# A decoder block with gathered and dense experts: gate loads and gate products held in the order of the program, and four steps of the gathered experts given high priority

## The chip, the cores and the metric

The kernel runs on one core of one Trainium2 chip. The metric is device time in microseconds (us) for one execution: the median of three runs for the time, one further profiled execution for the trace.

## The reference

One decoder layer for 1024 tokens of width 1024, in fp32. Three attention branches (stick-breaking, dilated windows, memory) are gated and summed, and their output projection is added to `x`; an expert layer follows, with 16,384 experts of which each token takes 16 for each of 8 heads:

```
sc = jnp.einsum('thpd,hpkd->thpk', q, subkeys)       # two lists of 128 keys per head
top_s, pos = lax.top_k(cand, PEER_TOPK)              # 16 of 16 x 16 sums of keys
gate = jax.nn.softmax(top_s, axis=-1)
act = jax.nn.gelu(jnp.einsum('chkd,cd->chk', u[ic], hc))
w = gate * act
out = jnp.einsum('chk,chkd->cd', w, v[ic])           # added to x
```

## The kernel before

The tokens are eight tiles of 128. Attention and the choice of experts run in three groups (`GROUPS` 2, 3, 3). For the expert layer there are two ways.

**Gathered tiles.** Six tiles go through `Experts`. For each of a token's 128 experts POOL starts an indirect DMA that gathers one row of `u` for each token (`fetch`, 128 x 1024, 512 KB); DVE multiplies it by `h` and sums it into a column of `parts` (L1315). After 32 such columns, a quarter `b` of the tile, come the steps that the change speaks of: ACT's gelu (`gelu`), DVE's multiplication by the gate factor `gk` (`scale`, L1329), PE's transposes and DVE's copy `wT` (`turn`, L1335), and DVE's spread weights `wz` for eight columns at a time (`weights`, L1339). POOL gathers rows of `v`, and PE multiplies four of them at a time by `wz` into the accumulators `poa` and `pob` (`sum`, L1349). In the last quarter the residual's piece `row` is loaded by SP (L1360), DVE adds the accumulator to it (L1362), and ACT stores it. `u` has 5 row buffers, `v` has 8, `wz` 2 and `row` 1.

**Dense tiles.** Tiles 4 and 6 (`DENSE`), 256 tokens, go through `dense()`: all 128 groups of 128 experts are computed, whatever was chosen. A matrix of gate factors, built earlier and stored in memory as `gd`, makes the result the reference's. For group `e`, `product` computes `w` = gelu(u h) with `u` split by ACT and DVE into a high and a low part (tiles `pu`, `pv` or `sc`, L1471). `weigh` then multiplies `w` by the gates of the group on DVE (L1552, the gate product), has ACT round it to `wh` and DVE subtract it to `wl` (L1557). PE multiplies `wh` and `wl` with the parts of `v` into eight banks (L1373). Two groups lie in one load of `ur` (uT) or `vr` (vd), 1 MB; one block `g` of gates, 1 MB for eight groups, has two buffers and is loaded by `gate_load`, called in the middle of the block before. Products of `u` are computed `RUN` = 22 groups ahead of the product with `v`, so that up to 24 `w` tiles are held. All loads go through `load` on SP (L242).

**What sets the order.** A planner in Python interleaves the gathered experts with everything else as it writes the program, by estimated costs of PE and of bytes. ACT and POOL issue in that written order. PE, DVE and SP are ordered by a scheduler, which may move an instruction ahead of others where its inputs and its buffers permit; `keep_in_program_order` holds an instruction behind the one written before it on its engine, and `high_priority` lets the scheduler take it as soon as it is ready by its own model of time.

Of the kernel before, what the change touches and what calls it, by code (L numbers as in the profile page):

```python
# [54 lines left out]
QB = 8  # L55
# [27 lines left out]
def block_kernel(ctx: ExitStack, tc: tile.TileContext, io):  # L83
    nc = tc.nc
# [12 lines left out]
    spread = keep.tile([128, QB, 32], BF, bufs=1)  # L97
# [29 lines left out]
    def actf(out, in_, f, **kw):  # L127
        s = SETS.get(f)
        if s and table[0] != s:
            nc.scalar.preload_act_table_set(s)  # L130
            table[0] = s
        nc.scalar.activation(out, in_, f, **kw)  # L132
# [40 lines left out]
    gofs, gwid, gnum, o = [], [], [], 0  # L173
# [58 lines left out]
    gd = dram.tile([TD // 32, 128, 128, 32], F32, name="gd")  # L232

    def count(ap):
        n = 4.0
        for d in ap.shape:
            n *= d
        moved[0] += n

    def load(out, src):  # L240
        count(out)
        nc.sync.dma_start(out, src)  # L242

    BR = ((0, 4), (4, 2), (6, 4))
    AHEAD_GATES = [(i // 3, i % 3) for i in range(12)]
# [49 lines left out]
    class Weights:  # L295
# [5 lines left out]
        def prepare(self):  # L301
            e = next(self.order, None)
            if e is None:
                return
            key, i, ks, split = e
            w = wp.tile([128, 8, 128], F32, name="w")
            w = w[:, :ks.stop - ks.start]
            load(w, io[key][i][:, ks])
            if split and key == "w_o":
                both_ = row_buffer("v").bitcast(F32R).rearrange("p (x k c) -> p x k c", x=2, c=128)  # L310
                w = halves(*(both_[:, x, :ks.stop - ks.start] for x in range(2)), w)
            elif split:
                w = halves(*(x.rearrange("p (k c) -> p k c", k=8) for x in spare()), w)
            self.ready.append((key, i, w))
# [108 lines left out]


    def opening(pipe, weights, hT, N):

        st = ExitStack()
# [12 lines left out]
        for k in range(0, KD, 4):  # L440
            load(memT[:, k:k + 4], io["memT"][:, k:k + 4])
            mem.append((row_buffer("v").bitcast(F32R).rearrange("p (k n) -> p k n", k=4), lows[:, k:k + 4]))
            for j in range(4):
                hi, lo = (x[:, j] for x in mem[-1])
                actf(hi, memT[:, k + j], AF.Copy, scale=g_mem[:, k + j:k + j + 1])
                nc.vector.scalar_tensor_tensor(lo, memT[:, k + j], g_mem[:, k + j:k + j + 1], hi, op0=OP.mult,
                                               op1=OP.subtract)
            weights.prepare()
        mem = None, mem
        load(hT[:, :, :N], io["xT"][:, :, :N])  # L450

        def square(k, x):
# [563 lines left out]
    coming = []  # L1016

    def select(pipe, weights, h2T, n0, G, out, scale):
        later = begin_input(G, GROUPS[1] * 128) if n0 == 0 else iter(())
        N = G * 128  # L1020
# [131 lines left out]
    def topk(n0, G, scs, out, lists, entry):  # L1152
        for i in range(G):
# [48 lines left out]
            for i4 in range(4):  # L1202
                turn(pt[:, i4 * 32:i4 * 32 + 32], idx[:, 32 * i4:32 * i4 + 32])
# [8 lines left out]
    def turn(out, src):  # L1212

        tok = ident.rearrange("p (c q j) -> p c q j", c=4, q=4)
        for q in range(4):
            mm(out[32 * q:32 * q + 32].rearrange("p (c j) -> p c j", c=4), src, tok[:, :, q, :],
               start=True, stop=True, skip_group_check=True)
# [32 lines left out]
    def quarters(dram_tile, c):  # L1250

        return [dram_tile[32 * c:32 * c + 32, 256 * k:256 * k + 256] for k in range(4)]

    class Experts:
# [71 lines left out]
            actf(t["ge"], t["parts"][:, 32 * b:32 * b + 32], AF.Gelu)  # L1326

        def scale(self, t, b):
            nc.vector.tensor_mul(t["ge"], t["ge"], t["gk"][:, 32 * b:32 * b + 32])  # L1329

        def turn(self, t):
            pt = pg.tile([128, 512], F32, name="pt")
            turn(pt[:, :32], t["ge"])
            t["w"] = gw.tile([128, 4, QB], F32, name="wT")
            nc.vector.tensor_copy(t["w"], pt[:, :32].rearrange("p (c j) -> p c j", c=4))  # L1335

        def weights(self, t, c):
            t["wz", c] = gw.tile([128, QB, 32], F32, name="wz")
            nc.vector.tensor_mul(t["wz", c], t["w"][:, c, :, None].to_broadcast([128, QB, 32]), spread)  # L1339

        def sum(self, t, b, c, j):
            if b == c == 0 and j == SUMS - 1:
                t["po"] = [pg.tile([128, 512], F32, name="po" + x) for x in "ab"]
            o = t["po"][c // 2][:, 256 * (c % 2):256 * (c % 2) + 256]
            vs = [self.vs.pop(0) for _ in range(SUMS)]
            for y in range(SUMS - 1, -1, -1):
                x = j - SUMS + 1 + y
                for k in range(4):
                    nc.tensor.matmul(o[32 * k:32 * k + 32], t["wz", c][:, x, :], vs[y][:, 256 * k:256 * k + 256],  # L1349
                                     start=b == 0 and x == SUMS - 1 and c % 2 == 0,  # L1350
                                     stop=b == 3 and x == QB - SUMS, skip_group_check=True)
            self.sums += SUMS
            if j == QB - 1 and c < 3:
                self.weights(t, c + 1)
            if b < 3:
                return
            if j == 3:
                t["row"] = gw.tile([128, 256], F32, name="row", bufs=1)
                for k, src in enumerate(quarters(xres[t["n"]], c)):
                    nc.sync.dma_start(t["row"][32 * k:32 * k + 32], src)  # L1360
            if j == QB - 1:
                nc.vector.tensor_add(t["row"], t["row"], o)  # L1362
                self.behind.append([None] * STORE + [lambda: self.store(t, c)])

        def store(self, t, c):
# [66 lines left out]
    def dense():  # L1432
# [41 lines left out]
        ur, us, ws, vr, gts = {0: first}, {}, {}, {}, {}  # L1474
# [30 lines left out]
        def gate_load(b):  # L1505
            if b < 16:
                gts[b] = dp.tile([128, TD // 32, 8, 32], F32, name="g")
                load(gts[b], gd[:, :, 8 * b:8 * b + 8, :].rearrange("b p i t -> p b i t"))

        e = steps = 0  # L1510
        while len(stored) < ND:
# [9 lines left out]
        while next(gates) < ND:  # L1521
# [5 lines left out]
            yield  # L1527
        hh, hl = split_tokens()
        gate_load(0)
        for e in range(e, RUN):  # L1530
            early(e)
# [16 lines left out]
        def weigh(e):  # L1548
            if e % 8 == 4:
                gate_load(e // 8 + 1)  # L1550
            w = ws.pop(e)
            nc.vector.tensor_mul(w.rearrange("p (b t) -> p b t", t=32), w.rearrange("p (b t) -> p b t", t=32),  # L1552
                                 gts[e // 8][:, :, e % 8, :])
            wh = da.tile([128, TD], F32R, name="wh", bufs=3)
            wl = da.tile([128, TD], F32R, name="wl", bufs=3)
            actf(wh, w, AF.Copy)
            nc.vector.tensor_sub(wl, w, wh)  # L1557
            return wh, wl

        take_v(0)  # L1560
        take_v(1)
        ready_w = [weigh(0), weigh(1)]
        for e in range(128):
            if e + RUN < 128:
                product(e + RUN, ab[:, e % 2, :])
                yield
            if e + 2 < 128:
                take_v(e + 2)
                ready_w.append(weigh(e + 2))
            (wh, wl), (vh, vl) = ready_w.pop(0), vs.pop(e)  # L1570
            for i in range(ND):
                c = slice(i * 128, (i + 1) * 128)
                for half in range(2):
                    o = sums[i][half]
                    f = slice(half * 512, (half + 1) * 512)
                    mmr(o, wh[:, c], vh[:, f], start=e == 0, stop=False, skip_group_check=True)
                    mmr(o, wh[:, c], vl[:, f], start=False, stop=False, skip_group_check=True)
                    mmr(o, wl[:, c], vh[:, f], start=False, stop=e == 127, skip_group_check=True)
                yield
# [47 lines left out]
    def fill(nside):  # L1627

        c, m = cost[0], moved[0]
        if next(filler[0], 0) == 0:  # L1630
            filler[0] = None
        spent = (cost[0] - c + 50) * slow[0], (moved[0] - m) / bw[0]
        c, m = cost[0], moved[0]
        credit[0] += nside * share[0]
        sides(int(credit[0]))
        credit[0] %= 1.0
        cost[0], moved[0] = c, m
        return spent
# [3 lines left out]
    while ex.done < NT - ND or filler[0] is not None:  # L1642
        if ex.more():
            least = LEAST * ((len(ex.todo) > 0) + (len(ex.vs) > 0))
            due = max(due + least, pe - least)
            while filler[0] is not None and (dma > pe or pe < due):
                a, b = fill(1)
# [7 lines left out]
        else:  # L1655
            a, b = fill(1)
            pe += a
            dma = max(dma + b, pe)
            c, m = cost[0], moved[0]
# [60 lines left out]
```

## Time and profile before

| | |
|---|---|
| median of 3 runs | 3528.4 us (3527.22 to 3533.35) |
| profiled execution | 3525.73 us, span 3524.0 us |
| mean granted TensorE clock | 0.947 |
| bytes moved | 1182.15 MB, mean 335 GB/s |
| DVE busy in gate products (L1552) | 52.2 us, 128 of them |
| first and last issue of a gate load on SP | 2610.5 and 3324.6 us |

The trace lists each engine's instructions with their start, and in brackets how long the engine had stood idle before one and what ended that. The chain is followed back from the last instruction, at each step to what released it. A busy share is an average over stages with different limits, so the prediction reads the stages apart. Line numbers are those of the kernel before; in the changed one they are up to 7 higher.

### The profile page before, as it was taken

To read this page: it belongs to the slowest core of one execution; us is meant where nothing else is said; L and a number is where in the kernel's file an instruction comes from. 1 tells how busy PE (TensorE), PEld (TensorE's weight loads), DVE (VectorE), ACT (ScalarE), POOL (GpSimd) and SP (SyncE) were. 2 spreads that over 40 slices of the span, in tenths; PEclk is the share of its full clock that TensorE was granted. 3 is DMA by queue.
4 is the path that set the end of the run, shared out by engine and by line. 5 is a ranking of instruction groups with operands and counts; after the bars stand their busy time and mean duration, and the time that the engine had idled before them with its cause. 6 is when DMAs were issued, how large, how long until landed. Compare 5 with 4: busy or idle time off the path is not lost.

```text
span 3524.0 us, 56887 instructions
## 1 busy us (share of the span) xinstructions
PE 3122.0 (89%) x21314; PEld 2268.7 (64%) x21314; DVE 2323.2 (66%) x5928; ACT 1062.8 (30%) x2135; POOL 1740.0 (49%) x1543
## 2 busy tenths in 40 slices
PE   8999978988999898889997999896878889998998
PEld 6888745655555474656564555574656767777776
DVE  7556788565454558887655665578769766676673
ACT  5674323332100111433322211111323333333332
POOL 0000156655566544556664565544665545555553
PEclk9999989999999999999997999897898999999999
DMA  5436789999899998789997999988999999999998
GB/s 186 127 108 191 269 301 327 375 335 366 288 387 407 410 363 320 268 311 334 384 352 267 344 382 388 389 303 320 377 406 357 356 394 400 406 409 394 409 400 311
DMA packets 345044, 1182.15 MB, mean 335 GB/s; under 512 B 38528, under 2 KB 81792, under 8 KB 325696
## 3 DMA queue, kind: packets, MB, share of 16 engines
q0 software_dynamic: 221184, 805.40, 60.5%
q1 hardware_dynamic: 100992, 336.37, 25.7%
q10 hardware_dynamic: 22592, 36.74, 2.8%
q8 instruction: 168, 2.75, 0.3%
q14 instruction: 108, 0.88, 0.1%
HBM read 1140.62 MB, written 37.75 MB: 334 GB/s over the span
## 4 chain that ended last, share of the span: by engine, by line
PE 48%; DMA 20%; DVE 14%; issue 9%; POOL 4%; ACT 3%; another core or an unknown queue 1%; ACTq 0%; SPq 0%; POOLq 0%; DVEq 0%
PE bank L121 32%; DMA u<-in_u,iI 11%; PE bank L1373 9%; DMA v<-in_v,iT 4%; PE poa L1349 4%; DVE u L1315 3%; PE pob L1349 3%; POOL u L1264 2%; POOL v L1264 2%; PE bank L125 1%; DMA vr<-in_vd 1%; DMA ur<-in_uT 1%; ACT e L132 1%; DMA g<-gd 1%
## 5 line engine op out<-in xcount | busy, mean ns | idle before, releaser
L1264 POOL DMA_INDIRECT u<-in_u,iI x768 | 878.9, 1144 | 977.0 <-DVE pos L1001 414.4
L1315 DVE SCALAR_TENSOR_TENSOR u<-u,h 128x1024 f32<-128x1024 f32 x768 | 932.2, 1219 | 484.7 <-DMA u<-in_u,iI 420.5
L1264 POOL DMA_INDIRECT v<-in_v,iT x768 | 860.3, 1120 | 773.0 <-PE pob L1349 288.9
L121 PE MATMUL bank<-wide,w 128*128 128x384 f32 x1536 | 525.1, 496 | 7.1 <-DMA w<-in_w_gate 7.1
L121 PEld LDWEIGHTS bank<-wide,w 128*128 128x128 f32 x1536 | 293.0, 194 | 213.1 <-issue 29.0
L1373 PE MATMUL bank<-hh,pu 128*128 128x256 f32 x1200 | 232.2, 294 | 37.6 <-ACT w L132 31.2
L132 ACT ACTIVATE e<-bank 128x512 f32<-128x512 f32 (+2 forms) x208 | 110.2, 530 | 493.5 <-PE bank L121 352.5
L1373 PE MATMUL bank<-pv,wh 128*128 128x512 f32 x712 | 232.0, 407 | 30.2 <-DVE pv L1471 21.3
L121 PE MATMUL bank<-big,w 128*128 128x256 f32 (+1 forms) x1280 | 241.3, 345 | 8.3 <-issue 8.1
L1349 PE MATMUL poa<-v,wz 128*32 128x256 f32 x3072 | 214.7, 400 | 26.9 <-DMA v<-in_v,iT 16.0
L121 PE MATMUL bank<-w,wide 128*128 128x128 f32 (+1 forms) x1056 | 223.8, 368 | 14.6 <-issue 6.0
L121 PEld LDWEIGHTS bank<-big,w 128*128 128x128 f32 x1280 | 208.8, 195 | 39.0 <-issue 18.2
L1373 PEld LDWEIGHTS bank<-hh,pu 128*128 128x128 f32 x1200 | 199.7, 201 | 51.3 <-ACT w L132 35.4
L1349 PE MATMUL pob<-v,wz 128*32 128x256 f32 x3072 | 205.9, 399 | 20.6 <-DMA v<-in_v,iT 14.1
L121 PEld LDWEIGHTS bank<-w,wide 128*128 128x128 f32 x1056 | 144.8, 193 | 89.0 <-issue 72.8
L1373 PEld LDWEIGHTS bank<-pv,wh 128*128 128x128 f32 x712 | 131.3, 193 | 69.3 <-DVE pv L1471 24.4
L1373 PE MATMUL bank<-hl,pu 128*128 128x256 f32 x600 | 174.5, 291 | 0.0
L1349 PEld LDWEIGHTS poa<-v,wz 128*32 128x32 f32 x3072 | 96.5, 113 | 117.1 <-issue 44.3
L1349 PEld LDWEIGHTS pob<-v,wz 128*32 128x32 f32 x3072 | 94.7, 113 | 113.7 <-issue 41.2
L132 ACT ACTIVATE w<-bank 128x256 f32<-128x256 f32 x128 | 48.8, 381 | 365.9 <-PE bank L1373 257.0
L1373 PE MATMUL bank<-v,u 128*128 128x256 f32 (+1 forms) x464 | 138.5, 299 | 10.5 <-ACT u L132 8.5
L132 ACT ACTIVATE pv<-vr 128x1024 fp32r<-128x1024 f32 x89 | 93.8, 1055 | 173.0 <-DMA vr<-in_vd 104.3
(333 smaller groups left out, 5692.3 us busy)
## 6 DMA issues: line engine op xcount, KB each, us to landing
ur<-in_uT SPq DMA_DIRECT2D x64, 1024.0 KB
vr<-in_vd SPq DMA_DIRECT2D x64, 1024.0 KB
w<-in_w_in SPq DMA_DIRECT2D x90, 512.0 KB
w<-in_w_gate SPq DMA_DIRECT2D x72, 512.0 KB
w<-in_w_pq SPq DMA_DIRECT2D x48, 512.0 KB
g<-gd SPq DMA_DIRECT2D x16, 1024.0 KB
w<-in_w_o SPq DMA_DIRECT2D x48, 256.0 KB
w<-in_w_out SPq DMA_DIRECT2D x24, 512.0 KB
```

What stands on the lines that cost most here:

```text
L121: nc.tensor.matmul(out, lhsT, rhs, **kw)
L125: nc.tensor.transpose(out, in_, ident)
L132: nc.scalar.activation(out, in_, f, **kw)
L1264: nc.gpsimd.indirect_dma_start(out=t, out_offset=None, in_=io[kind], in_offset=bass.IndirectOffsetOnAxis(ap=ap, axis=0))
L1315: nc.vector.scalar_tensor_tensor(u, u, 1.0, t["h"], op0=OP.mult, op1=OP.mult, accum_out=t["parts"][:, k:k + 1])
L1349: nc.tensor.matmul(o[32 * k:32 * k + 32], t["wz", c][:, x, :], vs[y][:, 256 * k:256 * k + 256], start=b == 0 and x == SUMS - 1 and c % 2 == 0,
L1373: nc.tensor.matmul(out, lhsT, rhs, **kw)
```

## The change

Three edits. A gate load, other than the first, and the gate product are held in program order. Four DVE operations of `Experts` are issued with high priority.

```diff
-    def load(out, src):
+    def load(out, src, tied=False):
         count(out)
-        nc.sync.dma_start(out, src)
+        i = nc.sync.dma_start(out, src)
+        if tied:
+            tc.keep_in_program_order(i)
...
         def scale(self, t, b):
-            nc.vector.tensor_mul(t["ge"], t["ge"], t["gk"][:, 32 * b:32 * b + 32])
+            with tc.high_priority():
+                nc.vector.tensor_mul(t["ge"], t["ge"], t["gk"][:, 32 * b:32 * b + 32])
...
-            nc.vector.tensor_copy(t["w"], pt[:, :32].rearrange("p (c j) -> p c j", c=4))
+            with tc.high_priority():
+                nc.vector.tensor_copy(t["w"], pt[:, :32].rearrange("p (c j) -> p c j", c=4))
...
-            nc.vector.tensor_mul(t["wz", c], t["w"][:, c, :, None].to_broadcast([128, QB, 32]), spread)
+            with tc.high_priority():
+                nc.vector.tensor_mul(t["wz", c], t["w"][:, c, :, None].to_broadcast([128, QB, 32]), spread)
...
             if j == QB - 1:
-                nc.vector.tensor_add(t["row"], t["row"], o)
+                with tc.high_priority():
+                    nc.vector.tensor_add(t["row"], t["row"], o)
...
-                load(gts[b], gd[:, :, 8 * b:8 * b + 8, :].rearrange("b p i t -> p b i t"))
+                load(gts[b], gd[:, :, 8 * b:8 * b + 8, :].rearrange("b p i t -> p b i t"), tied=b > 0)
...
-            nc.vector.tensor_mul(w.rearrange("p (b t) -> p b t", t=32), w.rearrange("p (b t) -> p b t", t=32),
-                                 gts[e // 8][:, :, e % 8, :])
+            tc.keep_in_program_order(
+                nc.vector.tensor_mul(w.rearrange("p (b t) -> p b t", t=32), w.rearrange("p (b t) -> p b t", t=32),
+                                     gts[e // 8][:, :, e % 8, :]))
```

Every engine keeps the same set of instructions. ACT and POOL keep their order; 18 of SP's 652 instructions, 485 of DVE's 4582 and 203 of PE's 13,706 stand elsewhere.

**SP at the dense start.** The loads of the dense tiles, from the eight `ur` loads of the first groups on, before:

```order
L242 DMA ur<-in_uT 128x2048 x8
L242 DMA g<-gd 128x8x256 x2
L242 DMA ur<-in_uT 128x2048
L242 DMA vr<-in_vd 128x2048
L242 DMA ur<-in_uT 128x2048
L242 DMA vr<-in_vd 128x2048
L242 DMA g<-gd 128x8x256
```

and in the changed kernel:

```order
L242 DMA ur<-in_uT 128x2048 x8
L242 DMA g<-gd 128x8x256
L242 DMA ur<-in_uT 128x2048
L242 DMA vr<-in_vd 128x2048
L242 DMA ur<-in_uT 128x2048
L242 DMA vr<-in_vd 128x2048
L242 DMA ur<-in_uT 128x2048
L242 DMA vr<-in_vd 128x2048
L242 DMA g<-gd 128x8x256
```

The second gate block, which stood directly behind the first, is now behind six loads of `ur` and `vr`.

**DVE in the middle of the dense stage**, from a `wz` that stands at 2834 us in the trace of before (`u,parts<-u,h` is a gathered row's product):

```order
L1339 TENSOR_TENSOR wz<-wT,spread 128x256
L1552 TENSOR_TENSOR w<-w,g 128x256 x4
L1315 SCALAR_TENSOR_TENSOR u,parts<-u,h 128x1024
L1552 TENSOR_TENSOR w<-w,g 128x256 x6
L1315 SCALAR_TENSOR_TENSOR u,parts<-u,h 128x1024
L1471 TENSOR_TENSOR pv<-vr,pv 128x1024
L1557 TENSOR_TENSOR wl<-w,wh 128x256
```

and in the changed kernel, from the same `wz`:

```order
L1344 TENSOR_TENSOR wz<-wT,spread 128x256
L1559 TENSOR_TENSOR w<-w,g 128x256
L1564 TENSOR_TENSOR wl<-w,wh 128x256
L1477 TENSOR_TENSOR pu<-ur,pu 128x1024
L1317 SCALAR_TENSOR_TENSOR u,parts<-u,h 128x1024 x2
L1477 TENSOR_TENSOR pv<-vr,pv 128x1024
L1559 TENSOR_TENSOR w<-w,g 128x256
L1564 TENSOR_TENSOR wl<-w,wh 128x256
```

Ten gate products stood there ahead of their turn; now each stands just ahead of the `wl` of its own group.

**SP at the end.** The last loads of `vr`, with the residual pieces of the last gathered tile, before:

```order
L242 DMA ur<-xres 128x1024
L242 DMA vr<-in_vd 128x2048 x5
L1360 DMA row<-xres 32x256 x4
L242 DMA vr<-in_vd 128x2048 x2
L1360 DMA row<-xres 32x256 x4
```

and in the changed kernel:

```order
L242 DMA ur<-xres 128x1024
L242 DMA vr<-in_vd 128x2048 x2
L242 DMA g<-gd 128x8x256
L242 DMA vr<-in_vd 128x2048 x3
L1365 DMA row<-xres 32x256 x4
L242 DMA vr<-in_vd 128x2048
L242 DMA g<-gd 128x8x256
L242 DMA vr<-in_vd 128x2048
L1365 DMA row<-xres 32x256 x4
```

The last two gate blocks, before issued at 3266.6 and 3324.6 us, now stand between these `vr` loads.

## The prediction

> **What bounds the kernel now.** I read the page first, then a table by stages of the last quarter, since the gate loads and gate products stand only there.
>
> ```profile
> PE 3122.0 (89%) x21314; PEld 2268.7 (64%) x21314; DVE 2323.2 (66%) x5928; ACT 1062.8 (30%) x2135; POOL 1740.0 (49%) x1543
> ...
> PE 48%; DMA 20%; DVE 14%; issue 9%; POOL 4%; ACT 3%; another core or an unknown queue 1%; ACTq 0%; SPq 0%; POOLq 0%; DVEq 0%
> ```
>
> The first line has the engines' busy time, the second the shares of the chain that ended last. PE leads both, but a fifth of the chain is DMA, so no stage can be priced by PE alone. In the next table the columns are the stretch, its length, then the busy time of PE, PEld, DVE, ACT and POOL with their instructions, the clock, the share of the DMA engines and GB/s.
>
> ```profile
> 2600.00:2660.00 60.00, 38.62 (x270) 29.90 (x267) 31.13 (x64) 15.17 (x23) 29.33 (x24) 0.80 1.02 400
> 2660.00:2760.00 100.00, 81.19 (x573) 66.19 (x569) 98.25 (x311) 33.75 (x50) 53.14 (x39) 0.88 0.85 321
> 2760.00:2940.00 180.00, 162.03 (x1191) 134.99 (x1192) 125.72 (x204) 59.10 (x92) 98.33 (x81) 0.95 1.02 401
> 2940.00:3330.00 390.00, 360.59 (x2664) 301.77 (x2663) 269.19 (x410) 145.96 (x225) 208.26 (x174) 0.98 1.02 403
> 3330.00:3430.00 100.00, 95.24 (x710) 79.25 (x709) 70.62 (x109) 34.90 (x54) 55.71 (x48) 0.98 1.01 400
> 3430.00:3524.00 94.00, 85.10 (x597) 59.68 (x596) 38.07 (x56) 27.14 (x42) 33.39 (x33) 0.97 0.82 318
> ```
>
> Five stages. The dense start (2600 to 2660) and the stretch from 2760 to 3430 have the DMA engines full, at 400 GB/s: there a byte that goes elsewhere is time. From 2660 to 2760 DVE is full (98 of 100 us, the last tile's lists), and DMA has room. After 3430 PE is busy 85 of 94 us and DMA has room again.
>
> **The dense start.** The queue of SP, then DVE, ACT, and the chain, in one fence each (start, length, what; idle time before it in brackets):
>
> ```profile
> 2610.51 5.67 SPq L242 DMA_DIRECT2D g<-gd  x2
> 2616.28 9.49 SPq L242 DMA_DIRECT2D ur<-in_uT  x1
> ```
>
> ```profile
> 2629.96 1.10 DVE L1552 TENSOR_TENSOR w<-w,g 128x256 f32<-128x256 f32 x3 [3.81 <-DMA g<-gd]
> ...
> 2647.19 1.23 DVE L1471 TENSOR_TENSOR pu<-ur,pu 128x1024 fp32r<-128x1024 f32 x1 [14.33 <-ACT pu L132]
> ```
>
> ```profile
> 2646.11 1.06 ACT L132 ACTIVATE pu<-ur 128x1024 fp32r<-128x1024 f32 x1 [14.94 <-DMA ur<-in_uT]
> ```
>
> ```profile
> 2616.28 29.73 DMA ur<-in_uT
> ```
>
> Two gate blocks are issued one after the other, the second waiting until 2615.8, and the load `ur` that ACT, DVE and the chain need goes out behind it. The first block lands at 2629.96 at the latest, `ur` at 2646.0. So between them the queue moved the second block and `ur`, 1 MB each, in 16.1 us: 8.0 us for one.
>
> **Term 1, SP's order at the dense start.** The second gate block now stands six loads later, so `ur` is not behind it. Gain 8.0 us, since the wait for `ur` is on the chain and ACT and DVE stand idle 14 us for it. Ends: 14.3 us if all of DVE's idle time goes, and 2.8 us, an estimate for the case that only the earlier issue counts (half of the 5.67 us for which the two gate issues hold SP). I take 8.0, between them, because it is measured for the same bytes on the same queue. The Trainium skill has a rule for such a mix of queues (DMA: Bandwidth & Descriptors, section Queues, rings and completion order): a ring is served in order, and an engine alternates between the rings that have work. By it, an estimate: half of 400 GB/s beside the gathers is 5.2 us for 1.05 MB, and the sum below would be 2.8 us smaller. The trace's 8.0 us is slower than such an even share.
>
> What becomes late next is DVE's list work from 2660 on. It is full there and starts from the same wait, so it moves forward with it; the second block's MB lands in the stretch where the DMA share is 0.85, and I cost it at nothing. Without that cover it is 2.6 us (1.05 MB at 400 GB/s).
>
> **Term 2, the gate products no longer run ahead.** DVE pulled them up to 22 experts forward, and the loads with them:
>
> ```profile
> 2759.78 0.43 SPq L242 DMA_DIRECT2D g<-gd  x1
> ...
> 2824.72 0.38 SPq L242 DMA_DIRECT2D g<-gd  x1
> ...
> 2922.83 0.38 SPq L242 DMA_DIRECT2D g<-gd  x1
> ```
>
> ```profile
> 2829.89 0.42 DVE L1552 TENSOR_TENSOR w<-w,g 128x256 f32<-128x256 f32 x1 [5.20 <-DMA g<-gd]
> ...
> 2849.58 1.10 DVE L1552 TENSOR_TENSOR w<-w,g 128x256 f32<-128x256 f32 x3 [11.69 <-DMA g<-gd]
> ```
>
> ```profile
> 2824.72 24.84 DMA g<-gd
> ```
>
> ```profile
> 2820.00:2860.00 40.00, 23.54 (x148) 18.83 (x147) 23.11 (x41) 7.96 (x12) 14.32 (x13) 0.83 1.01 388
> ```
>
> Six gate loads fall into 2760 to 2940 (the rows are the first, the third and the sixth), and two products hold DVE 16.9 us for blocks which no matmul needs for another 70 us or more (their products' places in the changed order). PE loses 16.5 of 40 us there, and the chain runs through that load for 24.84 us. Laying the changed order over these times, three of the six go later than 2940. But the DMA engines are full at 388 GB/s even while DVE stands, so only the bytes return: 3 x 1.05 MB / 401 GB/s = 7.8 us. Ends: 16.5 us (all of PE's idle time, if the gathers, held up by DVE, lose no bandwidth) and nothing (if PE's other waits fill it). I take 7.8, by the rate of the row.
>
> **Term 3, where the bytes go.** From 2940 to 3330 there are seven gate loads before and seven after. The last three, formerly before 3330, now stand at about 3384, 3431 and 3467. The one before 3430 meets full engines: 2.6 us. The two after it meet a share of 0.82, but there the chain waits for gathers of `v`:
>
> ```profile
> 3466.57 10.74 DMA v<-in_v,iT
> ...
> 3489.79 10.93 DMA v<-in_v,iT
> ```
>
> Half of 5.2 us for these two: together 5.2 us lost. Ends: 2.6, and 7.8 for all three in full.
>
> **Term 4, the product becomes a link between DVE and ACT.** Per expert DVE multiplies `w` by the gate, ACT rounds the result to `wh`, and DVE subtracts to `wl`. Now the product stands just ahead of `wl` on DVE, often next to it:
>
> ```profile
> L1552 DVE TENSOR_TENSOR w<-w,g 128x256 f32<-128x256 f32 x128 | 52.2, 419 | 22.4 <-DMA g<-gd 20.7 <-ACT w L132 1.7
> L132 ACT ACTIVATE wh<-w 128x256 fp32r<-128x256 f32 x128 | 51.8, 405 | 40.4 <-DVE w L1552 33.9 <-PE bank L1373 6.5
> ```
>
> ```profile
> DVE u L1315 <- DMA u<-in_u,iI: 118.1, 62, 5.6
> ...
> PE bank L1373 <- ACT w L132: 24.7, 8, 7.5
> ...
> PE bank L1373 <- DVE pv L1471: 5.5, 6, 1.3
> ```
>
> The second fence is the waits from 2940 to 3430 (total, times, longest). The number of products is the same; what is added is waiting. Behind a waiting product on DVE stand `wl`, the low parts `pv` and `pu`, and the row products of the gathers, which hold `u` buffers and so POOL; behind a waiting `wh` on ACT stand the next high parts and the gelu. DVE waits 62 times for a gathered `u`, 1.9 us on average, and whatever stands behind now includes a product for which ACT waits. In this stretch PE waits 14 times for either. I take one more wait of 1.9 us, 2 us, since DVE is idle 121 of 390 us from 2940 to 3330 and the 0.82 us of product and rounding fit there. Ends: nothing, and 14 further waits, 27 us.
>
> **Term 5, high priority.** The multiplication by the gate factor, `wT`, `wz` and the residual addition move up to 39 us forward on DVE; PE's sums follow in four places (near 750, 1880, 2670 and 2690); on SP one load of a weight block goes behind a residual load, 6 us later, and one load of `h` 8 us earlier.
>
> ```profile
> L1349 PE MATMUL poa<-v,wz x3072: 376/379/637, 527.7 to 3471.9; 128*32 128x256 f32 x192
> L1349 PE MATMUL pob<-v,wz x3072: 376/379/637, 579.0 to 3503.2; 128*32 128x256 f32 x192
> ...
>   DMA v<-in_v,iT: 30.1, 11
> ```
>
> ```profile
> L1339 DVE TENSOR_TENSOR wz<-wT,spread 128x256 f32<-128x256 f32 x96 | 39.0, 419 | 31.1 <-PE bank L121 17.1 <-PE poa L1349 10.8 <-remote 2.8
> ```
>
> PE waits 11 times for `v` before a sum, 2.7 us each; a sum that is moved forward past its gather waits once more, four groups: up to 11 us lost. `wz` waits for sums that free its two buffers: 10.8 us in six waits, so an earlier place may also stall DVE. On the other side, earlier sums free `v` buffers earlier, and what four groups may lose they may win. One multiplication goes to where ACT's gelu before it ends 2.3 us later, on a DVE that is full:
>
> ```profile
> 2721.78 0.22 ACT L132 ACTIVATE gel<-parts 128x32 f32<-128x32 f32 x1
> ```
>
> Its new place is 2719.7, the gelu's end 2722.0. I take 0, from -11 to +13. The last residual addition moves by one expert only, and the tail's row stores with it: nothing, as the chain there is `v` and the dense matmuls.
>
> **Sum:** -8.0 - 7.8 + 5.2 + 2.0 + 0 = -8.6 us against the profiled execution's 3525.7 (span 3524.0 and 1.7 around it), 3517.1. The median of the runs is 2.7 us above that execution, so the forecast for the median is 3519.8, a change of 0.24%. What a measurement tells from no change is about 0.2%, 7 us: faster means below 3521.3, slower above 3535.5.
>
> **Rivals.** A, slower: the product couples the engines. ACT's rounding waits for a product behind a row product that waits for a gather, ACT's next high part is late, and PE waits. For it speak the 62 waits and PE's 14; against it the idle time on DVE. Without term 4 the sum is -10.6, so it decides from six such waits of 1.9 us. With 12, as many as nearly all that PE has now: -10.6 + 22.8 = +12.2, 3540.6.
>
> B, late gate blocks at the end. The last two loads stand behind `vr` loads that wait for buffers:
>
> ```profile
> 3431.03 4.37 SPq L242 DMA_DIRECT2D vr<-in_vd  x2
> ```
>
> ```profile
> 3447.55 1.22 DVE L1471 TENSOR_TENSOR sc<-vr,sc 128x1024 fp32r<-128x1024 f32 x1
> ...
> 3483.49 1.23 DVE L1471 TENSOR_TENSOR pv<-vr,pv 128x1024 fp32r<-128x1024 f32 x1 [0.86 <-ACT pv L132]
> ```
>
> The block of expert 112 goes behind the first of these two, at 3431.4, and its product behind the first DVE row, at 3448.8: 17.4 us. For expert 120 it is 17.3 us to 3484.7. Landing took 19.4 us at 2610 and 24.8 at 2825. At 24.8 both are 7.4 late, so -8.6 + 14.9 = +6.3, 3534.7; below 21.7 us this gain stays. The Trainium skill's advice to double-buffer (Trainium Kernel Development and Optimization, section Best Practices) speaks against the shorter distance; two buffers remain here, and no run so far shows a load that late.
>
> C, no change: the engines are full from 2760 to 3430, PE's other waits take up terms 1 and 2, and only the order of the bytes is different: 3528.
>
> D, more gain: the sums moved forward free the gathers' buffers, term 5 at -11: 3508.8.
>
> **Chances.** The forecast 0.42 (two thirds of it under 3521.3), A 0.21, B 0.11, C 0.14, D 0.12. Faster: 0.28 + 0.12 + a little of B = 0.42; slower: A, and 0.04 of B with one of term 5's bad places = 0.26; the same: 0.32. The range reaches to A and to a little beyond D: 3505 to 3541. The forecast's own range is 3511 to 3527.
>
> **What would show it.** Term 1: ACT's wait for `ur` near 2630 falls from 14.9 to about 7 us. Term 2: no DVE wait on a gate block between 2760 and 2860, and PE there busy over 34 of 40 us. Term 3: the last block issued near 3460, with at most a short wait on it. Term 4: PE's waits for `w` and `pv` after 2940 grow by few. Term 5: the gate loads start within 5 us of 2610. Wrong would be: the dense start moved by over 5 us, or ACT's waits for the product at over 60 us together with more PE idle time.

## The result, and the profile after

The change makes the kernel slower: 3562.8 us against 3529.7 us (medians of six runs each), a ratio of 1.0070 with a 95% interval of 1.0042 to 1.0099. The forecast was 3519.8 us, and the range 3505 to 3541. Chips differ by over 1% here (the kernel before took 3529.7 to 3567.7 us as the median of its runs on four occasions), so the times below are told as ratios to the kernel before on the same chip. Waits and stages are read from one profiled execution of each kernel.

The page of the changed kernel (engines' busy time; shares of the chain):

```profile
PE 3148.4 (89%) x21314; PEld 2284.8 (64%) x21314; DVE 2334.8 (66%) x5928; ACT 1062.7 (30%) x2135; POOL 1742.9 (49%) x1543
...
PE 44%; issue 17%; DMA 16%; DVE 11%; POOL 7%; ACT 3%; another core or an unknown queue 2%; ACTq 0%; SPq 0%; POOLq 0%; DVEq 0%
```

DMA has less of the chain than before (16% against 20%), and PE is busy 26 us longer with the same matmuls. The first four rows of the table by stages, with the columns of the prediction's:

```profile
2600.00:2660.00 60.00, 45.00 (x295) 33.90 (x288) 37.28 (x90) 16.17 (x24) 33.50 (x29) 0.83 1.03 412
2660.00:2760.00 100.00, 81.21 (x591) 63.27 (x591) 96.98 (x292) 33.36 (x50) 44.72 (x38) 0.91 0.88 338
2760.00:2940.00 180.00, 161.07 (x1142) 136.04 (x1142) 121.04 (x182) 60.26 (x93) 97.05 (x79) 0.94 0.99 387
2940.00:3330.00 390.00, 348.51 (x2539) 290.00 (x2538) 259.81 (x388) 135.28 (x208) 204.54 (x165) 0.97 0.98 380
```

The dense start is better (PE 45.0 of 60 us against 38.6), and after 2940 PE does less in the same time: 2539 matmuls in 390 us where it did 2664. DMA, full there before at 403 GB/s, is at 380. A bound that gives way is a sign that another wait has come ahead of it.

ACT and POOL have the same order in both kernels, so an instruction of theirs can be compared with itself. By ACT's instructions the changed kernel is 0.6 us early at 2597, 13.6 early at 2646, 6.8 at 2728, 14.4 at 2868, and 31.9 us late at 3494. So it gains about as forecast up to 2870, and then loses 46 us. Single points are rough: between 2794 and 2894 the lead goes from 5 to 18 us and back to 2.

**The dense start**, SP and ACT of the changed kernel:

```profile
2607.92 0.38 SPq L242 DMA_DIRECT2D g<-gd  x1
2610.71 0.34 SPq L242 DMA_DIRECT2D ur<-in_uT  x1
...
2653.49 0.43 SPq L242 DMA_DIRECT2D g<-gd  x1
```

```profile
2632.54 1.06 ACT L132 ACTIVATE pu<-ur 128x1024 fp32r<-128x1024 f32 x1 [1.66 <-DMA ur<-in_uT]
```

ACT's wait for `ur` is 1.7 us, from 14.9.

**The stage that lost.** The waits of the changed kernel between 2882 and 3510 us, which is the same work as 2895 to 3484 before: 628 us against 589.

```profile
2882.00:3510.00 628.00, 566.40 (x4118) 464.41 (x4117) 405.10 (x613) 213.33 (x328) 330.68 (x271) 0.97 0.98 380
```

```profile
ACT wh L132 <- DVE w L1559: 293.8, 76, 10.4
DVE u L1317 <- DMA u<-in_u,iI: 133.9, 51, 6.7
...
PE bank L1379 <- ACT w L132: 55.0, 26, 5.0
```

The same stretch of the kernel before:

```profile
2895.00:3484.00 589.00, 552.71 (x4115) 455.06 (x4113) 394.94 (x603) 212.69 (x329) 320.25 (x271) 0.98 1.02 402
```

```profile
ACT w L132 <- PE bank L1373: 209.8, 61, 6.9
DVE u L1315 <- DMA u<-in_u,iI: 131.3, 67, 5.6
...
PE bank L1373 <- ACT w L132: 24.7, 8, 7.5
```

In the kernel before, ACT's longest wait in all is for PE's bank: ACT is ahead of PE. In the changed kernel it is for DVE's product: ACT is behind DVE. PE's idle time grows from 36.3 to 61.6 us, by 25; its waits for ACT's gelu alone grow by 30 (26 waits, from 8). PE's busy time grows by 13.7 us for the same work, at a mean clock of 0.97 against 0.98. How one wait is handed on, DVE, ACT and PE of the changed kernel:

```profile
3095.33 1.23 DVE L1317 SCALAR_TENSOR_TENSOR u<-u,h 128x1024 f32<-128x1024 f32 x1 [1.99 <-DMA u<-in_u,iI]
...
3097.62 0.42 DVE L1559 TENSOR_TENSOR w<-w,g 128x256 f32<-128x256 f32 x1
```

```profile
3098.13 0.42 ACT L132 ACTIVATE wh<-w 128x256 fp32r<-128x256 f32 x1 [7.59 <-DVE w L1559]
3098.46 1.04 ACT L132 ACTIVATE pu<-ur 128x1024 fp32r<-128x1024 f32 x1
3099.40 0.36 ACT L132 ACTIVATE w<-bank 128x256 f32<-128x256 f32 x1
```

```profile
3099.82 0.50 PE L1379 MATMUL bank<-hh,sc 128*128 128x256 f32 x2 [2.11 <-ACT w L132]
```

The product stands on DVE behind a gathered row's product, for whose row DVE waits 2.0 us, and behind a low part. ACT's rounding waits 7.6 us for it, and the high part and the gelu, `w<-bank`, come after it in ACT's written order. PE's next product with `u` needs the half bank that the gelu empties: PE has stood for 2.1 us when the gelu ends.

Such a wait can cost PE more than its own length. One of 4.9 us, with the clock in the 7 us around and behind it (column 0.51) and in the 7 us after those:

```profile
2924.95 0.80 PE L1379 MATMUL bank<-hh,pu 128*128 128x256 f32 x2 [4.91 <-ACT w L132]
2925.54 0.41 PE L1379 MATMUL bank<-hl,pu 128*128 128x256 f32 x1
```

```profile
2924.00:2931.00 7.00, 6.05 (x32) 5.58 (x36) 6.59 (x10) 3.74 (x7) 0.00 (x0) 0.51 0.87 312
2931.00:2938.00 7.00, 7.00 (x67) 5.62 (x56) 3.91 (x7) 2.17 (x3) 4.91 (x6) 1.00 0.92 323
```

The matmul takes 0.41 us there, and 0.28 us in the median of the stage. In the stage of 628 us the trace's clock records show a granted clock of 0.5 for 41.0 us in 11 pieces, each at a wait of PE for the gelu of 2.2 us or more (two waits as long have none); before there were 20.5 us in 4 pieces. An estimate from these: half of the 20.5 us more, 10 us, is lost to the clock, most of the 13.7.

### The profile page after: what moved, and what is told of

Its sections match the earlier page's. It is cut to its first block, busy times and chain, and to the rows that moved or that the text cites. A ratio compares the mean times of both kernels' runs of the same rounds, so it can differ in the third digit from the quotient of the medians.

```text
span 3555.8 us, 56872 instructions
## 1 busy us (share of the span) xinstructions
PE 3148.4 (89%) x21314; PEld 2284.8 (64%) x21314; DVE 2334.8 (66%) x5928; ACT 1062.7 (30%) x2135; POOL 1742.9 (49%) x1543
## 4 chain that ended last, share of the span: by engine, by line
PE 44%; issue 17%; DMA 16%; DVE 11%; POOL 7%; ACT 3%; another core or an unknown queue 2%; ACTq 0%; SPq 0%; POOLq 0%; DVEq 0%
PE bank L121 29%; DMA u<-in_u,iI 9%; PE bank L1379 8%; POOL u L1266 4%; DMA v<-in_v,iT 3%; POOL v L1266 3%; PE poa L1354 3%; DVE u L1317 3%; PE pob L1354 3%; PE bank L125 1%; ACT e L132 1%; DMA vr<-in_vd 1%; DVE v L287 1%; DMA w<-in_w_pq 1%
## 5 line engine op out<-in xcount | busy, mean ns | idle before, releaser
L1266 POOL DMA_INDIRECT v<-in_v,iT x768 | 869.3, 1132 | 853.5 <-PE pob L1354 320.3
L1379 PE MATMUL bank<-hh,pu 128*128 128x256 f32 x1200 | 239.5, 300 | 53.7 <-ACT w L132 47.8
L1354 PE MATMUL poa<-v,wz 128*32 128x256 f32 x3072 | 222.5, 410 | 36.4 <-DMA v<-in_v,iT 26.9
L121 PE MATMUL bank<-w,wide 128*128 128x128 f32 (+1 forms) x1056 | 223.7, 369 | 10.6 <-DVE wide L351 4.9
L132 ACT ACTIVATE wh<-w 128x256 fp32r<-128x256 f32 x128 | 53.4, 417 | 517.6 <-DVE w L1559 462.3
L1379 PE MATMUL bank<-u,v 128*128 128x256 f32 (+1 forms) x448 | 137.3, 307 | 3.9 <-ACT u L132 2.9
```

The lines of the kernel that those rows point to most:

```text
L121: nc.tensor.matmul(out, lhsT, rhs, **kw)
L1266: nc.gpsimd.indirect_dma_start(out=t, out_offset=None, in_=io[kind], in_offset=bass.IndirectOffsetOnAxis(ap=ap, axis=0))
L1379: nc.tensor.matmul(out, lhsT, rhs, **kw)
```

## The experiments

Three theories were stated first. Theory 1: the product directly ahead of the subtraction makes a ring of DVE and ACT, as told above (the prediction's rival A). Theory 2: the gate blocks' bytes and their late place cost the time (rival B with term 3). Theory 3: the high priority does.

**The parts one by one.** Four kernels, on one chip: without the pinned product, only the product pinned, only the loads pinned, and without priority. The edits, in this order (each the changed kernel with):

```diff
-            tc.keep_in_program_order(
-                nc.vector.tensor_mul(w..., gts[e // 8][:, :, e % 8, :]))
+            nc.vector.tensor_mul(w..., gts[e // 8][:, :, e % 8, :])          # no_product
...
-                load(gts[b], gd[...], tied=b > 0)
+                load(gts[b], gd[...])                                        # product_alone, with no_prio
...
-            with tc.high_priority():                                        # no_prio (four places);
                                                                             # load_alone: no_prio and no_product
```

> The change without the pinned gate product: loads pinned, high priority kept, the product free to run ahead on DVE (about 8 groups, as far as its gate block is loaded). Theory 1 (coupling): the 45 us that the change lost after 2944 us come from ACT's rounding waiting for a product that now stands directly before the subtraction; without it ACT waits for the product under 80 us in all and the time is 3505 to 3522 us, below before. Theory 2 (the late gate blocks and their bytes at the end): nothing comes back, about 3560. Theory 3 (high priority): about 3560.

> Only the gate product pinned; loads and priorities as before. Theory 1: ACT waits for the product some 400 us in over 100 places, PE waits for ACT's gelu twice as often as before, 3550 to 3570. Theory 2: the loads are free to go early, so no loss, 3520 to 3530. Theory 3: 3520 to 3530.

> Only the gate loads pinned; products free, no priorities. Theory 1: the gain of the dense start and of the bytes not brought forward stays, 3508 to 3522. Theory 2: the loss stays, 3550 or more. Theory 3: as theory 1.

> Loads and product pinned, no high priority. Theory 1: as the change within 8 us, 3555 to 3570. Theory 2: the same. Theory 3 (high priority costs the time): 3515 to 3530.

| | ratio to before | 95% interval | ACT waits for the product | PE waits for the gelu | DVE waits for a gate block |
|---|---|---|---|---|---|
| before | 1 | | 34 us, 6 | 35 us, 9 | 21 us, 3 |
| the change | 1.0070 | 1.0042 to 1.0099 | 462 us, 116 times | 67 us, 33 times | 4 us |
| no_product | 1.0084 | 1.0054 to 1.0114 | 35 us, 7 | too short to be listed | 113 us, 14 |
| product_alone | 1.0121 | 1.0087 to 1.0155 | 496 us, 117 | 79 us, 25 | 4 us |
| load_alone | 1.0077 | 1.0053 to 1.0101 | 44 us, 8 | 4 us, 4 | 117 us, 14 |
| no_prio | 1.0090 | 1.0056 to 1.0123 | 442 us, 111 | 64 us, 29 | 4 us |

All four are slower, and Theory 1 as stated had two of them wrong: without the pinned product (no_product, load_alone) the time did not come back. The waits show why. Where the product is pinned, PE waits for the gelu. Where only the loads are pinned, that wait is gone, and another has come:

```profile
DVE w L1554 <- DMA g<-gd: 117.0, 14, 16.5
PE bank L1375 <- DVE pv L1473: 46.2, 10, 7.2
ACT wh L132 <- DVE w L1554: 44.0, 8, 11.4
```

These are waits of load_alone over the whole execution. A free product runs ahead until it meets a block that is still on its way, 14 times, and DVE, which issues in order, stands there up to 16.5 us with the low parts for PE behind it. Before, it did so three times, for 20.7 us, as the loads ran further ahead, too. So the two pins seem to have a loss each, and taking out the one brings up that of the other: Theory 4, which is argued from these waits. High priority is not the cause (no_prio is as slow), so Theory 3 falls; product_alone is slow with loads free, so Theory 2 can't be the only cause.

**The ring taken apart.** If the ring is the loss, it is enough to make the product a little earlier, still pinned, so that neither the loads run far ahead nor ACT waits. `gate` has the load and the product, and `weigh` calls it for a later group:

```diff
+        def gate(e):
+            if e > 127:
+                return
+            if e % 8 == 4:
+                gate_load(e // 8 + 1)
+            w = ws[e]
+            tc.keep_in_program_order(nc.vector.tensor_mul(w..., gts[e // 8][:, :, e % 8, :]))
...
         def weigh(e):
-            if e % 8 == 4:
-                gate_load(e // 8 + 1)
             w = ws.pop(e)
-            tc.keep_in_program_order(nc.vector.tensor_mul(w..., gts[e // 8][:, :, e % 8, :]))
...
             actf(wh, w, AF.Copy)
             nc.vector.tensor_sub(wl, w, wh)
+            gate(e + 1)                       # ahead3_noprio: e + 3, ahead2_noprio: e + 2
             return wh, wl
...
+        for e in range(1):                    # 3 and 2
+            gate(e)
         ready_w = [weigh(0), weigh(1)]
```

The kernels named noprio leave the four priorities out. prio_alone is another kind: the change with both pins taken out, so that only the priorities are left.

> The change with one thing moved: the gate product of a group is written, and pinned, one group earlier, behind the subtraction of the group before, so that ACT's rounding finds it done; the gate load is called one group earlier with it. Theory 1 (ring of DVE and ACT): ACT's waits for the product fall from 294 us after 2880 to under 60, PE's waits for ACT's gelu from 55 to under 30, and the time is 3510 to 3530, not slower than before. Theory 2 (what costs is that products no longer run ahead by 20 groups, with the loads and bytes that belong to it): the distance of one group changes nothing, 3555 to 3570.

> Pinned product and loads three groups earlier, without high priority. Theory 1: as one group earlier, 3510 to 3530, ACT's waits for the product under 20 us. Theory 2: a little better than one group, 3550 to 3565.

> Pinned product and loads one group earlier, without high priority. Theory 1: 3510 to 3530 and within 8 us of the same with priority. Theory 2: 3555 to 3570.

> Only the high priority of the four DVE operations; products and loads free as before. Theory 1: the same as before within 10 us, since the loss comes from the product and the load. Theory 3 (priority has a cost or a gain of its own before 2600 us): beyond 10 us either way.

> Product and loads pinned two groups earlier, no priority. Theory 1: ACT's waits for the product under 60 us, PE's for the gelu under 10; the time 3510 to 3530, as with one group, since PE's waits for the gelu are gone already there.

| | ratio to before | 95% interval | ACT waits for the product | PE waits for the gelu | DVE waits for a gate block |
|---|---|---|---|---|---|
| ahead1 | 0.9974 | 0.9954 to 0.9995 | 201 us, 62 | 6 us, 2 | 5 us |
| ahead1_noprio | 0.9967 | 0.9941 to 0.9993 | 226 us, 69 | 6 us, 3 | 4 us |
| ahead2_noprio | 0.9986 | 0.9965 to 1.0007 | 28 us, 8 | 7 us, 4 | 4 us |
| ahead3_noprio | 0.9989 | 0.9962 to 1.0015 | 9 us, 1 | 4 us, 2 | 4 us |
| prio_alone | 0.9996 | 0.9970 to 1.0021 | 36 us, 5 | 33 us, 8 | 17 us, 3 |

ahead2_noprio ran on another chip than the other four. One group takes the whole loss back: 1.0070 becomes 0.9974, each beside the kernel before on its chip, some 34 us, with every instruction and every priority of the change. The gate loads go one group earlier with the product (the last one is issued at 3470 us, in the change at 3498), so this run alone does not exclude Theory 2; round_dve, below, has the loads where the change has them. What I expected of ACT's wait was wrong: it fell to 152 us after 2895, not under 60, and the time came back all the same.

```profile
ACT wh L132 <- DVE w L1561: 201.1, 62, 9.4
PE bank L1379 <- DVE pv L1477: 14.8, 5, 6.5
PE bank L1379 <- ACT w L132: 6.4, 2, 4.2
```

In these waits of ahead1 ACT still waits 201 us for the product, and PE almost never for ACT. So what counts in these kernels is not how long ACT waits, but whether the gelu behind it is late for PE. From one group to three ACT's wait falls to 9 us, and the ratio doesn't fall with it (the intervals overlap). The priorities alone are worth nothing that these runs can tell, and the residual's addition, `wT` and `wz` with them.

**Another hand for the rounding.** The product stays where the change has it, and DVE rounds, so that the ring has one engine:

```diff
-            actf(wh, w, AF.Copy)
+            nc.vector.tensor_copy(wh, w)
             nc.vector.tensor_sub(wl, w, wh)
```

> The change with the rounding to wh done on DVE instead of ACT, the product where the change has it: nothing goes from DVE to ACT and back, and DVE has 128 x 0.42 = 54 us more work. Theory 1 (ACT's queue stands behind the rounding, and with it the gelu that frees PE's bank): PE's waits for the gelu fall from 67 us to under 15, and the time is 3520 to 3540, back near before in spite of the work added. Rival (the product's place on DVE itself is what costs, whoever rounds): 3560 or more.

The ratio was 0.9991 (0.9973 to 1.0009). PE's waits for the gelu fell to 17 us, six times (under 15 was expected), and the loss of the whole was gone, some 28 us, though the new roundings come to some 54 us on DVE, an estimate of 128 at 0.42 us each. On SP the order is that of the change, but for one load of a residual piece, so Theory 2 falls here:

```profile
2903.00:3512.00 609.00, 566.58 (x4109) 459.18 (x4108) 419.16 (x702) 184.82 (x241) 304.46 (x270) 0.97 1.00 394
```

This is the stage that took 628 us in the changed kernel. On the same chip as this run ahead2_noprio took 594 us for the same work, so some 15 us are still lost in it; PE waits 32 us for the rounding and the subtraction, which now both stand on DVE (27 times). So it is mainly ACT standing for the product that costs; whether the rest is the product's late place or the work added on DVE is not shown.

**Gate loads earlier, products free.** To take the wait of Theory 4 away, the loads were called eight groups ahead instead of four:

```diff
-            if e % 8 == 4:
+            if e % 8 == 0:
                 gate_load(e // 8 + 1)
```

> Loads pinned but called eight groups ahead of the block instead of four, products free, no priority. Theory 4 (in the two kernels with pinned loads and free products the loss is DVE standing at a product that runs ahead to a block still on its way): DVE's waits for gate blocks fall from 117 us to under 40, and the time is 3520 to 3540. Rival (pinning the loads costs by their bytes at the end): 3555 to 3570.

The ratio was 1.0070 (1.0043 to 1.0098), and DVE still waited 99 us in 13 places for gate blocks. The wait was not removed, so neither Theory 4 nor its rival is decided by this run; the second block also went out 5 us behind the first again. What speaks for Theory 4 is the pair load_alone and ahead3_noprio: loads pinned in both, the product free or pinned three groups ahead, 117 or 4 us of waiting for blocks, 1.0077 or 0.9989. The loads stand three groups earlier in ahead3_noprio, but four groups earlier, in load_early, did not help, so the loads alone do not explain the loss. That the wait itself costs it remains argued.

**The loads free again.** ahead1_noprio with `tied` left out, so that SP may issue the second block behind the first; SP also moves later blocks and some other loads by a few places:

> Product pinned one group earlier as before, loads not pinned, no priority: only the second block goes out behind the first again. Term 1 of the prediction: it takes back the gain at the dense start, so 6 to 10 us slower than the same with pinned loads, 3520 to 3530. Rival (the second block's place is worth nothing, as other transfers fill it): within 4 us.

The ratio was 1.0019 (0.9997 to 1.0042), against 0.9967 (0.9941 to 0.9993) with the loads pinned; the two were on different chips, each beside the kernel before. ACT's row at the dense start, without the pinned loads and with them:

```profile
2685.86 1.06 ACT L132 ACTIVATE pu<-ur 128x1024 fp32r<-128x1024 f32 x1 [14.05 <-DMA ur<-in_uT]
```

```profile
2626.77 1.06 ACT L132 ACTIVATE pu<-ur 128x1024 fp32r<-128x1024 f32 x1 [1.75 <-DMA ur<-in_uT]
```

The wait of 14 us comes back with the second block's early place, as term 1 has it. The difference of the ratios, 0.5%, is 18 us and more than the 6 to 10 us expected; PE's waits for the gelu also rose from 6 to 34 us in this kernel, so it is not all of one cause. The same pin makes the difference between product_alone and no_prio, on one chip: 1.0121 against 1.0090, 0.3% or 11 us, with intervals that overlap.

## Why the prediction was wrong

**Term 1 (-8.0) had the mechanism right, and its nearness to what remained is in part luck.** From the issue of `ur` to ACT's row it was 29.8 us before and is 21.8 now: 8.0 us, as the term has it. But `ur` is also issued 3.0 us sooner behind the first block, which the term took for another way to count and not for an addend, and the first block itself goes out 2.6 us sooner; together the 13.6 us of ACT's row, and the wait fell to 1.7 us, not to 7. Of the 13.6 us, 6.8 remained at 2728, though the prediction let DVE's list work move forward whole. What took the other half is not shown; DVE is full there (97 of 100 us). The even shares of the Trainium skill (DMA: Bandwidth & Descriptors, section Queues, rings and completion order) gave 5.2 us, an estimate; the rows' 8.0 us for the block is more.

**Term 2 (-7.8) was right in what it names.** The two waits on gate blocks there are gone, three gate loads are left between 2760 and 2940 instead of six, and from 2728 to 2868 the changed kernel went from 6.8 to 14.4 us early. As the lead jumps by more than 10 us from one instruction to the next there, this is no measurement of the 7.8.

**Term 3 (+5.2) is not contradicted, and not measured.** In ahead1_noprio, which has late loads without the ring, the gathers are 19.9 us early at 3330 and 12.8 at 3483, but the lead goes down to 9.3 and up to 19.6 between. In the changed kernel DVE waits once for a gate block, 3.6 us at the dense start and nowhere at the end, so rival B did not happen.

**Term 4 (+2.0) is the step that failed.** It put one further wait of 1.9 us on the ring. The stage took 39 us more; taking the ring apart gave back 34 us (ahead1) and 28 us (round_dve). So the ring costs some 30 us. Of the stage's 39 us, 25 are idle time of PE and 14 its longer busy time, some 10 of these by the clock of 0.5 at its waits, a cost that no term had. The prediction's sign of being wrong, ACT's waits for the product at over 60 us together with more PE idle time, came at 462 us. I had both facts, the 62 waits of DVE for gathers and that the gelu stands behind the rounding, and named the mechanism as rival A with 22.8 us at a chance of 0.21; even that was too little (3540.6 us), and it put the delay on the next high part, where the runs show the gelu. What was wrong was the sizing: I counted how often PE waited before, 14 times, and took the idle time of DVE as room. But most of DVE's idle time from 2940 to 3430, 118 of 150 us, is there *because* it waits for gathers, and what stands behind such a wait on DVE, the product included, is late by it. Also, how far the ring reaches PE is not seen from the waits before, since the products then ran ahead and ACT seldom had to stand for one: 34 us in six places.

**Term 5 (0) was right:** with the priorities alone the ratio is 0.9996, and ahead1 with and without them agrees.

**What the forecast left out** is that pinning the loads without the product would have lost as well (1.0077). Where PE's waits for the gelu and DVE's for blocks are both small and the loads stay pinned, the ratios are 0.9967, 0.9974, 0.9986 and 0.9989. The sum without term 4, -10.6 us, would be 0.9970. Only the first two intervals exclude no change, and each of them is 0.4% to 0.5% wide, so a gain of that kind is shown, and its size is not.

## What to carry to other kernels

Before pinning an operation between two engines, look at what stands behind its consumer on that engine's queue, and at what its producer waits for ahead of it; here the operation placed one step earlier cost nothing that these runs can tell, and PE's waits for the gelu were nearly gone. Holding back a load and holding back its use belong together: here a use that ran ahead to a block on its way held DVE for up to 16.5 us, with PE's low parts behind it. And a long wait of an engine is to be judged by whether the bound engine waits for it: 201 us of ACT's waiting had no price that shows, while the loss came with PE's waits for the gelu, 67 us instead of 35.

## What the runs showed of the hardware

A DMA share near 1.0 left room: in the stage after 2880 the changed kernel moved 380 GB/s at a share of 0.98, and before and with the product one or two groups ahead it was 400 to 403 GB/s at 1.01 to 1.02, so a share near 1 doesn't prove that DMA is what bounds. And the same matmuls did not always take PE the same time. In that stage, with nearly the same matmuls, PE was busy 552.7 us where its granted clock was 0.5 for 20.5 us (before), 556.9 with 27.3 us of it (ahead2_noprio), and 566.4 and 566.6 with 41.0 us (the changed kernel, round_dve). In the changed kernel each such piece stood at a wait of PE of 2.2 us or more.
